# The beginning of a hybrid DeltaNet and attention layer: another order for scaled tiles, low parts, modulation rows and their weights

## The chip, the cores and the metric

The kernel runs on one core of one Trainium2 chip. The metric is the device time of one execution in microseconds (us). A median of three executions is given, and the profile of one execution. The engines are TensorE (PE, matrix products; PEld is its loading of the stationary operand), VectorE (DVE), ScalarE (ACT), GpSimd (POOL) and SyncE (SP, which issues most of the DMAs).

## The reference

One layer of a diffusion backbone over 1024 latent tokens and 256 context tokens, 1024 features wide. The part that the change touches is the start of it:

```
mod_x = silu(c) @ w_ada + b_ada          # shift, scale, gate, twice, for latent tokens
mod_c = silu(c_ctx) @ w_ada + b_ada      # the same for context tokens
px = modulate(rms_norm(x,   norm1_w), sh1,  sc1)  @ w_in
pc = modulate(rms_norm(ctx, norm1_w), csh1, csc1) @ w_in
# modulate(h, shift, scale) = h * (1 + scale) + shift
```

The columns of the projection feed a gated DeltaNet (convolution over the sequence, two scans) and a neighbourhood attention. Then come the output projection, a gated residual, a second modulated norm, and a SwiGLU network with its residual. All in float32.

## The kernel before, in words

The 1280 tokens (256 of context first) lie along the free dimension; the 1024 features are eight tiles `k` of 128 partitions. Float32 products are made from a high part (`hh` of the activations, `whi` of the weights, in the fast fp32r type) and a low part (`hl`, `wlo`, what the high part leaves), as three products: `hh` with `whi`, `hl` with `whi`, `hh` with `wlo`.

The beginning runs in these steps:

- SP loads the eight tiles `xt` (L680), the two raw weight blocks `fraw` for the first two projection blocks (L684), then the modulation weights `wada`, 1 MB for each tile (L676), and constants between them.
- The sums of squares go over ScalarE and VectorE to TensorE (L737 to L742), and `rs`, the inverse root, is made on ScalarE (L744, L745).
- `first[0].prefetch` casts and splits the first raw block on VectorE; `first[1].prefetch` the second on GpSimd (L201 the cast to `whi`, L204 the subtraction that gives `wlo`).
- `ada(j)` makes the modulation row of tile `j` on TensorE (L706: 16 instructions, four abreast) and copies it from PSUM to `arow` (L708). `column(j)` turns the row into columns by small products with `sel` (L714), adds the bias and makes the scale `w1s` on VectorE (L716, L719).
- `normed_tile(k)` scales the tile in place on VectorE (L726), makes `hh` on ScalarE, which adds the shift (L727), then `hl` on VectorE (L729). It does so in pieces: 256, 512 and 512 tokens for tile 0, 256 and 1024 for the others.
- The first two projection blocks (`first`, the DeltaNet's first two heads of k) are accumulated together, tile after tile (L757 for tile 0, L413 for the others), each over three PSUM banks. `AHEAD` says after which block of which tile a further row or column is made.

PE, DVE and ACT run this part in the order in which it is written (`tc.manual_schedule`); SP and POOL are in queues of their own. After tile 7 the third block begins outside that part, where the compiler's scheduler orders the engines: `first[0].evac()` copies the first block's three banks on ScalarE with a scale (L446) and VectorE adds the convolution's other taps straight from PSUM (L455); `jobs[2].prefetch()` casts the third block's weights on ScalarE (L203) and splits them on GpSimd (L204). The pool of `whi` and `wlo` has two buffers each, so the third block's take those of the first. Beside the later blocks VectorE accumulates another part of the modulation (L236, L238).

Of the kernel before, what the change touches and what calls it, by code (L numbers as in the profile page):

```python
# [9 lines left out]
F32 = mybir.dt.float32  # L10
# [3 lines left out]
AF = mybir.ActivationFunctionType  # L14
# [5 lines left out]
D, L, CT, T = 1024, 1024, 256, 1280  # L20
KT = 8
# [12 lines left out]
C_ID, C_LE, C_GE, C_BD2, C_ONE = range(5)  # L34
# [18 lines left out]
WIN = (256, 0)  # L53
CTX = {256: slice(0, 256), 0: slice(384, 640)}
PACE = 0.66
AHEAD = {(1, 0): (3,), (1, 1): (3, 4), (2, 0): (4, 5), (2, 1): (5, 6, 7), (3, 0): (6, 7)}
ORDER = [list(range(NCH)), [1, 0] + list(range(9, 1, -1))]


# [29 lines left out]
def hybrid(ctx, tc, a, dbg):  # L89
    nc = tc.nc  # L90
    pe, act, dve, pool, sp = nc.tensor, nc.scalar, nc.vector, nc.gpsimd, nc.sync
# [18 lines left out]
    bias = lasting("bias", [128, 8])  # L110
# [14 lines left out]
    M = [cst[:, i * 128:(i + 1) * 128] for i in range(4)] + [ones]  # L125
# [32 lines left out]
    mod1 = const("mod1", [128, 16, 2])  # L158
# [224 lines left out]
    with ExitStack() as bs:  # L383
# [7 lines left out]
        def bank(name="m"):  # L391

            if len(psum) == 1:
                return psum[0].tile([128, 512], F32, name=name, tag="ps")
            if len(psum) == 2:
                return psum[1].tile([128, 512], F32, name=name, tag=name, bufs=4 if name == "blk" else 2)
            return psum[2].tile([128, 512], F32, name=name, tag="ps", bufs=2)

        hh, hl = [], []
# [265 lines left out]
        first = [Block("k", 0), Block("k", 1)]  # L665
        with ExitStack() as xs:
            xp = pools(xs, "xp", "left")
            xt = []
            masks = xp.tile([128, 4, 128], F32, name="masks", tag="masks")
            ascope = ExitStack()  # L670
            wap = pools(ascope, "wap", "right", 7)
            aw = {}

            def load_ada(j):
                aw[j] = w = wap.tile([128, KT, 256], F32, name="wada", tag="wada")
                sp.dma_start(w, a["wa1"][j])  # L676

            for k in range(KT):
                x = xp.tile([128, T], F32, name=f"xt{k}", tag=f"xt{k}")
                sp.dma_start(x, a["xcT"][k])  # L680
                xt.append(x)
            raws = [xp.tile([128, KT, 128], F32, name=f"fraw{i}", tag=f"fraw{i}") for i in range(2)]
            for i in range(2):
                sp.dma_start(raws[i], a["w_conv"][4 + i])  # L684
            for j in range(3):
                load_ada(j)
            sp.dma_start(cst, a["cst"])
            sp.dma_start(masks, a["masks"])
            for j in range(3, KT):
                load_ada(j)  # L690
            sp.dma_start(cw, a["cw"])
            sp.dma_start(qkw, a["qkw"])
            sp.dma_start(onw, a["onw"])
            sp.dma_start(adt, a["adt"].rearrange("o d -> (o d)").partition_broadcast(128))
            wide = xp.tile([128, KT, 32], F32, name="wide", tag="wide")
            pool.memset(wide, 0.0)
            pool.tensor_copy(wide[:, :, 0:2], sc2)
            rs = xp.tile([128, T], F32, name="rs", tag="rs")
            rows = {}

            def ada(j, copy):

                p, w = bank("pm"), aw.pop(j)
                for k in range(KT):
                    s = slice(32 * (k % 4), 32 * (k % 4) + 32)
                    pe.matmul(p[s, :256], wide[:, k], w[:, k], start=k < 4, stop=k >= 4)  # L706
                rows[j] = xp.tile([128, 256], F32, name="arow", tag="arow", bufs=2)
                copy(rows[j], p[:, :256])  # L708

            def column(j):  # L710

                p, row = bank("pm"), rows.pop(j)
                for b in range(2):
                    pe.matmul(p[:, 2 * b:2 * b + 2], row[:, b * 128:(b + 1) * 128], sel, start=True, stop=True)  # L714
                m = mod1.rearrange("p (s b) c -> p s b c", s=2)[:, :, j]
                dve.tensor_tensor(m, p[:, 0:4].rearrange("p (s c) -> p s c", s=2),  # L716
                                  bada[:, 0:16].rearrange("p (s b) -> p s b", s=2)[:, :, j:j + 1].to_broadcast(
                                      [128, 2, 2]), OP.add)
                dve.tensor_scalar(w1s[:, j], m[:, 1], 1.0, n1w[:, j:j + 1], op0=OP.add, op1=OP.mult)  # L719

            def normed_tile(k, cuts=(slice(0, CT), slice(CT, T))):
                t = xt[k]
                parts = [(x, mod1[:, k, int(x.start < CT):int(x.start < CT) + 1]) for x in cuts]
                for x, sh in parts:
                    j = int(x.start < CT)
                    dve.scalar_tensor_tensor(t[:, x], t[:, x], w1s[:, k, j:j + 1], rs[:, x], op0=OP.mult, op1=OP.mult)  # L726
                    act.activation(hh[k][:, x], t[:, x], AF.Identity, bias=sh)  # L727
                for x, sh in parts:
                    dve.scalar_tensor_tensor(hl[k][:, x], t[:, x], sh, hh[k][:, x].bitcast(F32),  # L729
                                             op0=OP.add, op1=OP.subtract)  # L730

            with tc.manual_schedule(engines={mybir.EngineType.PE, mybir.EngineType.DVE, mybir.EngineType.Activation}):
                sums = [bank() for _ in SEGS]
                segs = [slice(s0, s0 + n) for s0, n in SEGS]
                for k in range(0, KT, 2):
                    sq = [xp.tile([128, T], F32, name="sq%d" % i, tag="sq%d" % i, bufs=2 + i) for i in range(2)]
                    act.activation(sq[0], xt[k], AF.Square)  # L737
                    for s in segs if k == KT - 2 else [slice(0, T)]:
                        act.activation(sq[1][:, s], xt[k + 1][:, s], AF.Square)
                        dve.tensor_tensor(sq[1][:, s], sq[0][:, s], sq[1][:, s], OP.add)  # L740
                    for p, s in zip(sums, segs):
                        pe.matmul(p[:, :s.stop - s.start], M[C_ONE], sq[1][:, s], start=k == 0, stop=k == KT - 2)  # L742
                for p, s in zip(sums, segs):
                    act.activation(rs[:, s], p[:, :s.stop - s.start], AF.Ln, bias=b_eps, scale=1.0 / D)  # L744
                act.activation(rs, rs, AF.Exp, scale=-0.5)  # L745
                first[0].prefetch(raws[0], dve, dve)
                first[1].prefetch(raws[1], pool, pool)
                ada(0, dve.tensor_copy)
                column(0)
                normed_tile(0, segs)  # L750
                ada(1, act.copy)
                for b in first:
                    b.banks()
                for j, (w, x) in enumerate(((0, hh), (1, hh), (0, hl))):
                    for b in first:
                        for o, s in b.outs:
                            pe.matmul(o, b.w[w][:, 0], x[0][:, s], start=j == 0, stop=False)  # L757
                        if j == 0 and b is first[1]:
                            column(1)
                            normed_tile(1)  # L760
                ada(2, act.copy)
                column(2)
                for k in range(1, KT):
                    if k == 3:
                        ascope.close()
                        h_tiles(pools(bs, "hp2", "right"), 4)
                    if k + 1 < KT:
                        normed_tile(k + 1)
                    for j, b in enumerate(first):
                        b.mm([k])  # L770
                        for q in AHEAD.get((k, j), ()):
                            if q in rows:
                                column(q)
                            else:
                                ada(q, act.copy)
                    if k == 5:
                        act.copy(mr[:, 4], ident)
                        act.copy(mr[:, 0:4], masks)
# [310 lines left out]
        for n in range(2, len(jobs) + 2):  # L1089
            j = jobs[n] if n < len(jobs) else None  # L1090
# [276 lines left out]
    parts = [[x[:, k] for k in range(4)] + [n[:, i] for n in na] for i, x in enumerate(ga)]  # L1367
# [130 lines left out]
    with ExitStack() as os_:  # L1498
# [21 lines left out]
        for b in range(2, KT - 2):  # L1520
            w, nxt = nxt, load_w(a["w_out"][b + 1], lo_engine=dve)
            sp.dma_start(x2[:, b], a["xcT"][b, :, CT:])
            outs = [bank(), bank()]
            for k in range(KT):
                for j, (wi, xi) in enumerate(((0, 0), (0, 1), (1, 0))):
                    for o, s in zip(outs, HV):
                        pe.matmul(o, w[wi][:, k], parts[xi][k][:, s], start=k == 0 and j == 0,  # L1527
                                  stop=k == KT - 1 and j == 2)
# [14 lines left out]
        for t, s in enumerate(HV):  # L1543
            outs = [bank(), bank()]
            last.append(outs)
            for k in range(KT):
                for j, (wi, xi) in enumerate(((0, 0), (0, 1), (1, 0))):
                    for o, w in zip(outs, ws):
                        pe.matmul(o, w[wi][:, k], parts[xi][k][:, s], start=k == 0 and j == 0,  # L1549
                                  stop=k == KT - 1 and j == 2)  # L1550
# [9 lines left out]
    with ExitStack() as us:  # L1560
# [66 lines left out]
        w = {}  # L1627
# [104 lines left out]
    for n, (wn, xn) in enumerate(zip(Stream.DOWN, FACTORS)):  # L1732
        o = chains[n in (1, 3, 5)]
# [90 lines left out]
```

## Time and profile before

| | us |
|---|---|
| median of 3 executions | 1516.04 |
| lowest, highest | 1512.98, 1517.41 |
| span of the profiled execution, first to last instruction | 1510.6 |
| own time of the profiled execution | not listed apart; its span stands for it |
| TensorE busy in it | 1462.2 |
| VectorE, ScalarE, GpSimd busy in it | 996.8, 703.5, 236.7 |

A row of the timeline gives the start in us from the first instruction, the duration, the engine, the line, the operation, the tiles written and read, the shape of the first one and the count of instructions merged into the row; in brackets the engine's idle time before it and what ended that. A row by stretches gives its length, the busy time of PE, PEld, DVE, ACT and POOL with counts of instructions, the granted share of TensorE's clock, the mean busy share of the DMA engines, and GB/s. A row of a group of instructions gives busy time, mean duration in ns, and idle time before with what ended it.

### The profile page before, as it was taken

What the parts mean: (1) busy time and instruction counts of PE and PEld (TensorE: products, weight loads), DVE (VectorE), ACT (ScalarE), POOL (GpSimd) and SP (SyncE); (2) the same over time, 40 slices, a digit from 0 to 9 for tenths busy, and PEclk for the clock granted to TensorE, in tenths of its full rate; (3) what the DMA queues carried; (4) which work ended last, traced back from release to release, by engine and by line L of the source; (5) the groups of instructions that cost most, each with busy time, mean ns of one, the idle gap of its engine ahead of it and who ended that gap; (6) DMA issues with size and microseconds to landing.
All of it is one profiled execution on the core that took longest, in us unless ns stands there. A gap on an engine that the chain in (4) does not pass through costs nothing.

```text
span 1510.6 us, 23890 instructions
## 1 busy us (share of the span) xinstructions
PE 1462.2 (97%) x8702; PEld 1223.5 (81%) x8702; DVE 996.8 (66%) x1716; ACT 703.5 (47%) x1389; POOL 236.7 (16%) x286
## 2 busy tenths in 40 slices
PE   6999999999999998999999999999999999999998
PEld 3788797877788877887878888888888888888887
DVE  5773589875463745778867389766665567598652
ACT  5453442456663246656853284333333334354440
POOL 1054601456652201111210000000000000000000
PEclk9999999999999999999999999999999999999999
DMA  9274122778665569998539205433333335798742
GB/s 389 75 215 143 54 78 72 244 222 248 195 191 174 157 187 291 290 263 279 163 112 343 79 28 166 141 105 105 105 105 105 105 105 174 260 360 279 251 140 84
DMA packets 205398, 267.36 MB, mean 177 GB/s; under 512 B 15968, under 2 KB 113760, under 8 KB 204256
## 3 DMA queue, kind: packets, MB, share of 16 engines
q1 hardware_dynamic: 197680, 260.01, 53.2%
q10 hardware_dynamic: 7600, 5.81, 1.2%
q8 instruction: 69, 1.13, 0.3%
q14 instruction: 49, 0.40, 0.1%
HBM read 201.02 MB, written 68.94 MB: 179 GB/s over the span
## 4 chain that ended last, share of the span: by engine, by line
PE 51%; ACT 1%; DVE 1%; issue 0%; DMA 0%; POOL 0%; DVEq 0%; POOLq 0%; ACTq 0%
PE ps L1398 28%; PE ps L1741 14%; PE ps L1527 3%; PE ps L1375 1%; PE ps L1549 1%; PE sc L332 1%; PE sc L322 1%; PE sc L309 1%; PE ps L1252 0%; PE ps L1261 0%; DMA z<-z_d 0%; ACT sq L1302 0%; ACT bt L315 0%; DVE bt L313 0%; PE ps L223 0%
## 5 line engine op out<-in xcount | busy, mean ns | idle before, releaser
L1459 ACT CAST uhi<-wq 128x512 fp32r<-128x512 f32 x101 | 61.3, 622 | 135.9 <-issue 84.6
L413 PE MATMUL blk<-hh,whi 128*128 128x512 f32 (+1 forms) x410 | 121.0, 389 | 1.6 <-ACT kk L562 1.4
L1459 ACT CAST uhi<-ws 128x512 fp32r<-128x512 f32 x91 | 54.0, 621 | 146.3 <-PE ps L1398 91.4
L413 PE MATMUL blk<-hl,whi 128*128 128x512 f32 (+1 forms) x410 | 113.4, 370 | 0.3 <-DVE hl L729 0.3
L609 PE MATMUL blk<-zw,hh 128*128 128x256 f32 (+1 forms) x576 | 112.3, 289 | 1.0 <-ACT cr L461 1.0
L413 PE MATMUL blk<-hh,wlo 128*128 128x512 f32 (+1 forms) x410 | 112.0, 370 | 0.6 <-POOL wlo L204 0.6
L1460 DVE TENSOR_TENSOR ulo<-wq,uhi 128x512 fp32r<-128x512 f32 x101 | 67.6, 688 | 59.1 <-ACT uhi L1459 32.7
L1398 PE MATMUL ps<-hT,uhi 128*128 128x512 f32 x336 | 103.7, 390 | 0.0
L1398 PE MATMUL ps<-lT,uhi 128*128 128x512 f32 x336 | 103.4, 389 | 0.0
L1398 PE MATMUL ps<-hT,ulo 128*128 128x512 f32 x336 | 103.4, 389 | 0.0
L609 PEld LDWEIGHTS blk<-zw,hh 128*128 128x128 f32 x576 | 90.7, 189 | 4.1 <-ACT cr L461 1.4
L1398 PE MATMUL ps<-hB,uhi 128*128 128x512 f32 x288 | 89.1, 390 | 0.0
L1398 PE MATMUL ps<-lB,uhi 128*128 128x512 f32 x288 | 88.7, 389 | 0.0
L1398 PE MATMUL ps<-hB,ulo 128*128 128x512 f32 x288 | 88.7, 389 | 0.0
L413 PEld LDWEIGHTS blk<-hh,wlo 128*128 128x128 f32 x410 | 71.0, 188 | 14.8 <-POOL wlo L204 0.9
L413 PEld LDWEIGHTS blk<-hl,whi 128*128 128x128 f32 x410 | 71.2, 188 | 14.4 <-DVE hl L729 0.8
L609 PE MATMUL blk<-zw,hl 128*128 128x256 f32 (+1 forms) x288 | 81.9, 284 | 0.0
L413 PEld LDWEIGHTS blk<-hh,whi 128*128 128x128 f32 x410 | 67.6, 190 | 16.8 <-issue 3.8
L204 POOL TENSOR_TENSOR wlo<-wraw,whi 128x1024 fp32r<-128x1024 f32 x18 | 44.8, 2488 | 186.8 <-ACT whi L203 186.5
L1398 PEld LDWEIGHTS ps<-lT,uhi 128*128 128x128 f32 x336 | 63.1, 188 | 13.1
L1398 PEld LDWEIGHTS ps<-hT,ulo 128*128 128x128 f32 x336 | 63.1, 188 | 13.1
L1398 PEld LDWEIGHTS ps<-hT,uhi 128*128 128x128 f32 x336 | 62.9, 188 | 13.0
(361 smaller groups left out, 3500.7 us busy)
## 6 DMA issues: line engine op xcount, KB each, us to landing
wq<-w_fo SPq DMA_DIRECT2D x99, 256.0 KB, 4.2
wq<-w_gu SPq DMA_DIRECT2D x88, 256.0 KB, 2.9
wad<-wa SPq DMA_DIRECT2D x64, 256.0 KB, 4.3
bt<-rpb SPq DMA_DIRECT2D x64, 192.0 KB, 3.9
t_d<-g SPq DMA_DIRECT2D x22, 512.0 KB, 3.5
fr<-t_d SPq DMA_DIRECT2D x44, 256.0 KB, 4.9
f_d<-g SPq DMA_DIRECT2D x33, 256.0 KB, 2.1
fr<-f_d SPq DMA_DIRECT2D x33, 256.0 KB, 4.2
```

The lines of the kernel that those rows point to most:

```text
L204: lo_engine.tensor_tensor(o, r, h.bitcast(F32), OP.subtract)
L309: s = pe.matmul(sc[:, u * 640 + n0:u * 640 + n1], q, ks[i], start=i == 0, stop=i == 1)
L322: pe.transpose(sc[:, u * 640 + j * 128:u * 640 + (j + 1) * 128], bt[:, j * 128:(j + 1) * 128], ident)
L332: pe.matmul(sc[u * ND:u * ND + ND, 1280:1408], vv, pt[:, j * 128:(j + 1) * 128], start=j == 0, stop=j == 4)
L413: pe.matmul(o, ww[:, k], xx[k][:, s], start=k == 0 and j == 0, stop=k == KT - 1 and j == 2)
L609: pe.matmul(p[:, :c1 - c0], x[k][:, s], ww[:, k, c0:c1], start=k == 0 and j == 0, stop=k == KT - 1 and j == 2)
L1375: pe.matmul(o, w[wi][:, k], parts[xi][k][:, s], start=k == 4 and j == 0, stop=k == 3 and j == 2)
L1398: pe.matmul(o, w[wi][:, k], x[xi][:, k], start=first and k == 0 and j == 0, stop=k == n - 1 and j == 2, skip_group_check=True)
L1459: act.copy(hi, self.raw[key])
L1460: dve.tensor_tensor(lo, self.raw[key], hi.bitcast(F32), OP.subtract)
L1527: pe.matmul(o, w[wi][:, k], parts[xi][k][:, s], start=k == 0 and j == 0, stop=k == KT - 1 and j == 2)
L1741: pe.matmul(o[b], w[wi][:, b], F[xn, p][xi], start=n in (0, 1, 5) and p == 0 and j == 0, stop=p == NFB // 2 - 1 and j == 2, skip_group_che ...
```

## The change

In SP's queue the first modulation weights are loaded ahead of the two raw weight blocks. `ada` takes a tuple of tiles and writes up to two rows into one PSUM bank, with one copy; tiles 4 and 5, and 6 and 7, are done by twos. `normed_tile` is split into `high` (scaling and `hh`) and `low` (`hl`); from tile 2 on, the next tile's `high` stands ahead of the present tile's `low`. The six groups of three products of a tile are in a new order: all four that need `hh` first, the two that need `hl` last. `busy(n)` issues n products of `ones` with a tile of squares into a bank that nobody reads, three between row 0 and column 0, two after column 0. The table `AHEAD` gives way to `behind`, which names a group instead of a block.

```diff
             raws = [xp.tile([128, KT, 128], F32, name=f"fraw{i}", tag=f"fraw{i}") for i in range(2)]
+            load_ada(0)
             for i in range(2):
                 sp.dma_start(raws[i], a["w_conv"][4 + i])
-            for j in range(3):
+            for j in (1, 2):
                 load_ada(j)
...
+            def ada(js, copy):
+
+                p = bank("pm")
+                for n, j in enumerate(js):
+                    w = aw.pop(j)
+                    for k in range(KT):
+                        s = slice(32 * (k % 4), 32 * (k % 4) + 32)
+                        pe.matmul(p[s, n * 256:n * 256 + 256], wide[:, k], w[:, k], start=k < 4, stop=k >= 4)
+                row = xp.tile([128, 512], F32, name="arow", tag="arow", bufs=2)
+                copy(row[:, :len(js) * 256], p[:, :len(js) * 256])
...
+            def high(k, cuts=whole):
                 t = xt[k]
+                for x in cuts:
                     j = int(x.start < CT)
                     dve.scalar_tensor_tensor(t[:, x], t[:, x], w1s[:, k, j:j + 1], rs[:, x], op0=OP.mult, op1=OP.mult)
+                    act.activation(hh[k][:, x], t[:, x], AF.Identity, bias=shifted(k, x))
+
+            def low(k, cuts=whole):
+                for x in cuts:
+                    dve.scalar_tensor_tensor(hl[k][:, x], xt[k][:, x], shifted(k, x), hh[k][:, x].bitcast(F32),
                                              op0=OP.add, op1=OP.subtract)
+
+            def part(b, k, w, x):
+                for o, s in b.outs:
+                    pe.matmul(o, b.w[w][:, k], x[k][:, s], start=k == 0 and w == 0 and x is hh,
+                              stop=k == KT - 1 and x is hl)
+
+            def busy(n):
+
+                for _ in range(n):
+                    pe.matmul(idle[:, :256], M[C_ONE], sq[0][:, :256], start=True, stop=True)
...
                 first[0].prefetch(raws[0], dve, dve)
                 first[1].prefetch(raws[1], pool, pool)
-                ada(0, dve.tensor_copy)
+                ada((0,), dve.tensor_copy)
+                busy(3)
                 column(0)
-                normed_tile(0, segs)
-                ada(1, act.copy)
+                busy(2)
+                high(0, segs)
+                low(0, segs)
+                ada((1,), act.copy)
                 for b in first:
                     b.banks()
...
+                one, two = first
+                part(one, 0, 0, hh)
+                column(1)
+                high(1)
+                part(one, 0, 1, hh)
+                part(two, 0, 0, hh)
+                part(two, 0, 1, hh)
+                ada((2,), act.copy)
+                part(one, 0, 0, hl)
                 column(2)
+                part(two, 0, 0, hl)
+                low(1)
+                high(2)
+                behind = {(1, 0): lambda: ada((3,), act.copy), (1, 2): lambda: column(3),
+                          (2, 2): lambda: ada((4, 5), act.copy), (2, 4): lambda: (column(4), column(5)),
+                          (2, 5): lambda: ada((6, 7), act.copy), (3, 3): lambda: (column(6), column(7))}
                 for k in range(1, KT):
...
-                    if k + 1 < KT:
-                        normed_tile(k + 1)
-                    for j, b in enumerate(first):
-                        b.mm([k])
-                        for q in AHEAD.get((k, j), ()):
...
+                    if k >= 2 and k + 1 < KT:
+                        high(k + 1)
+                    if k >= 2:
+                        low(k)
+                    for n, (b, w, x) in enumerate(((one, 0, hh), (one, 1, hh), (two, 0, hh), (two, 1, hh),
+                                                   (one, 0, hl), (two, 0, hl))):
+                        part(b, k, w, x)
+                        if (k, n) in behind:
+                            behind[k, n]()
```

More of the change, by code (lines that the diff above doesn't have):

```diff
@@ L699, in hybrid @@
             rows = {}
[L701 to L708, printed above, removed]
+            def ada(js, copy):
[7 more added lines that the diff above has]
+                copy(row[:, :len(js) * 256], p[:, :len(js) * 256])
+                for n, j in enumerate(js):
+                    rows[j] = row[:, n * 256:n * 256 + 256]
             def column(j):
@@ L719, in column, with shifted @@
                 dve.tensor_scalar(w1s[:, j], m[:, 1], 1.0, n1w[:, j:j + 1], op0=OP.add, op1=OP.mult)
-            def normed_tile(k, cuts=(slice(0, CT), slice(CT, T))):
+            whole = (slice(0, CT), slice(CT, T))
+            def shifted(k, x):
+                return mod1[:, k, int(x.start < CT):int(x.start < CT) + 1]
+            def high(k, cuts=whole):
                 t = xt[k]
-                parts = [(x, mod1[:, k, int(x.start < CT):int(x.start < CT) + 1]) for x in cuts]
-                for x, sh in parts:
+                for x in cuts:
                     j = int(x.start < CT)
                     dve.scalar_tensor_tensor(t[:, x], t[:, x], w1s[:, k, j:j + 1], rs[:, x], op0=OP.mult, op1=OP.mult)
-                    act.activation(hh[k][:, x], t[:, x], AF.Identity, bias=sh)
-                for x, sh in parts:
-                    dve.scalar_tensor_tensor(hl[k][:, x], t[:, x], sh, hh[k][:, x].bitcast(F32),
+                    act.activation(hh[k][:, x], t[:, x], AF.Identity, bias=shifted(k, x))
+            def low(k, cuts=whole):
+                for x in cuts:
+                    dve.scalar_tensor_tensor(hl[k][:, x], xt[k][:, x], shifted(k, x), hh[k][:, x].bitcast(F32),
                                              op0=OP.add, op1=OP.subtract)
+            def part(b, k, w, x):
[5 more added lines that the diff above has]
+                    pe.matmul(idle[:, :256], M[C_ONE], sq[0][:, :256], start=True, stop=True)
             with tc.manual_schedule(engines={mybir.EngineType.PE, mybir.EngineType.DVE, mybir.EngineType.Activation}):
@@ L745, in hybrid @@
                 act.activation(rs, rs, AF.Exp, scale=-0.5)
+                idle = bank()
                 first[0].prefetch(raws[0], dve, dve)
                 first[1].prefetch(raws[1], pool, pool)
-                ada(0, dve.tensor_copy)
+                ada((0,), dve.tensor_copy)
+                busy(3)
                 column(0)
-                normed_tile(0, segs)
-                ada(1, act.copy)
+                busy(2)
+                high(0, segs)
+                low(0, segs)
+                ada((1,), act.copy)
                 for b in first:
                     b.banks()
[L754 to L761, printed above, removed]
-                column(2)
+                one, two = first
[7 more added lines that the diff above has]
+                part(one, 0, 0, hl)
+                column(2)
+                part(two, 0, 0, hl)
[4 more added lines that the diff above has]
+                          (2, 5): lambda: ada((6, 7), act.copy), (3, 3): lambda: (column(6), column(7))}
                 for k in range(1, KT):
@@ L766, in hybrid @@
                         h_tiles(pools(bs, "hp2", "right"), 4)
-                    if k + 1 < KT:
-                        normed_tile(k + 1)
-                    for j, b in enumerate(first):
-                        b.mm([k])
-                        for q in AHEAD.get((k, j), ()):
[L772 to L775, printed above, removed]
+                    if k >= 2 and k + 1 < KT:
[7 more added lines that the diff above has]
+                            behind[k, n]()
                     if k == 5:
```

1 line of the change is left out of this document (removed).

## The prediction

> **What bounds the kernel now.** I read the page first, then the busy time by stretches of 10 and of 1 us over the beginning, then the timeline of the first 100 us. The page's head and its table of engines say that TensorE (PE) sets the pace:
>
> ```profile
> span 1510.6 us, 23890 instructions
> PE 1462.2 (97%) x8702; PEld 1223.5 (81%) x8702; DVE 996.8 (66%) x1716; ACT 703.5 (47%) x1389; POOL 236.7 (16%) x286
> ```
>
> TensorE sits idle for 48 us of the whole span, so what the change can win lies where TensorE waits or runs slowly in the edited stretch, from the first modulation row (21.8 us) to the first product of the third block (67.6 us). In the stretches of 1 us below, the number before the last two is the granted clock.
>
> ```profile
> 21.00:22.00 1.00, 0.24 (x5) 0.19 (x8) 0.58 (x1) 0.88 (x2) 1.00 (x1) 1.00 1.02 426
> 23.00:24.00 1.00, 0.58 (x4) 0.52 (x4) 0.37 (x1) 0.08 (x1) 0.80 (x1) 1.00 1.04 434
> 24.00:25.00 1.00, 0.81 (x9) 0.40 (x12) 0.80 (x4) 0.00 (x0) 0.00 (x0) 0.55 0.95 393
> 30.00:31.00 1.00, 1.00 (x5) 0.81 (x5) 0.96 (x3) 0.27 (x1) 0.00 (x0) 0.54 1.00 418
> ```
>
> TensorE is 0.24 and 0.58 busy, then the clock is halved just after 24.0 and comes back just before 31. The first products of the two blocks, from 26.1 on, run at half speed: 4.9 us that would take 2.4. That is the most the filler sums can win. The DMA engines are full (share about 1.0), at some 420 GB/s.
>
> **The change part by part.** The rows of the start, from the timeline (start, duration, engine, line; in brackets the idle time before and what ended it):
>
> ```profile
> 18.92 0.69 DVE L201 CAST whi<-fraw 128x1024 fp32r<-128x1024 f32 x1
> 19.24 1.26 POOL L201 CAST whi<-fraw 128x1024 fp32r<-128x1024 f32 x1 [13.63 <-DMA fraw<-w_conv]
> 19.64 1.94 DVE L204 TENSOR_TENSOR wlo<-fraw,whi 128x1024 fp32r<-128x1024 f32 x1
> 21.81 1.07 PE L706 MATMUL pm<-wada,wide 128*32 128x256 f32 x16 [0.76 <-DMA wada<-wa]
> 22.94 0.42 DVE L708 COPY arow<-pm 128x256 f32<-128x256 f32 x1 [1.36 <-PE pm L706]
> 23.42 0.61 PE L714 MATMUL pm<-bias,arow 128*128 128x2 f32 x4 [0.54 <-DVE arow L708]
> 24.22 1.94 PE L706 MATMUL pm<-wada,wide 128*32 128x256 f32 x16 [0.19 <-DMA wada<-wa]
> 24.59 1.81 DVE L726 SCALAR_TENSOR_TENSOR xt<-xt,w1s,rs 128x256 f32<-128x256 f32 x3
> 25.77 1.38 ACT L727 ACTIVATE hh<-xt,mod 128x512 fp32r<-128x512 f32 x2 [0.15 <-DVE xt L726]
> ```
>
> *First modulation weights sooner.* No transfer is added; the first `wada` (1 MB) passes the two `fraw` (0.5 MB each) on SP's queue, and later ones keep their places. `wada` 0 and 1 land 2.4 us apart (21.81, 24.22), so 1 MB costs 2.4 us: `wada` 0 lands near 19.3 instead of 21.8, both `fraw` 2.4 us later, the second near 21.65, the first half of that earlier, near 20.45. The row product can now start when the sums of squares leave TensorE, near 21.0, 0.8 us sooner. But VectorE does `whi` and `wlo` of the first block ahead of the row's copy: 0.69 from 20.45, then `wlo` for 1.1 to 1.9, to 22.3–23.1, and the copy 0.42. TensorE puts three filler sums between row and column; the row product's 16 instructions run four abreast in about a microsecond (rows below), some 0.22 for a pass of 256 columns, two passes to an f32 sum, so 1.3 for three. The column starts near 23.3, 0.1 sooner than now: the gain is nothing. What is late next is the second block's weights on GpSimd (POOL). Its cast goes from about 21.7 to 23.1, and `wlo` follows. Whether that matters is read from later rows of the same engines:
>
> ```profile
> 66.63 2.39 POOL L204 TENSOR_TENSOR wlo<-wraw,whi 128x1024 fp32r<-128x1024 f32 x1 [42.83 <-ACT whi L203]
> 81.02 2.88 POOL L602 TENSOR_TENSOR zw<-wraw,zw 128x1088 fp32r<-128x1088 f32 x1 [4.47 <-ACT zw L601]
> 81.43 0.75 DVE L455 SCALAR_TENSOR_TENSOR cacc<-blk,cw,cacc 128x512 f32<-128x512 f32 x1
> 82.09 2.36 DVE L238 SCALAR_TENSOR_TENSOR acc<-wad,sc,acc 128x512 f32<-128x512 f32 x1
> 85.03 0.73 DVE L238 SCALAR_TENSOR_TENSOR acc<-wad,sc,acc 128x512 f32<-128x512 f32 x1
> 92.99 3.52 DVE L238 SCALAR_TENSOR_TENSOR acc<-wad,sc,acc 128x512 f32<-128x512 f32 x1
> 93.02 2.96 POOL L566 TENSOR_TENSOR kd<-kk,cst 128x1280 f32<-128x1280 f32 x1 [0.88 <-ACT kk L562]
> ```
>
> The accumulation at L238 reads two SBUF tensors. Alone it takes 0.73; beside a GpSimd product it ends 0.5 us after that product does (82.09+2.36 against 81.02+2.88; 92.99+3.52 against 93.02+2.96). The form that reads PSUM (81.43) isn't held. So GpSimd's `wlo`, 23.2 to 25.6 after the change, holds VectorE's first scaling of tile 0, which reads `xt` and `rs` from SBUF: its first piece ends near 26.15 instead of 25.07, 1.1 us later. The other end is no hold, 0. I take 1.1; three rows stand nearest.
>
> [...]
>
> *Filler sums.* Five, 2.1 us on TensorE, in time when it waits for VectorE or ScalarE. They fill the idle stretches ahead of the drop, so I take the clock to stay up. The other end, that it falls all the same, is a rival.
>
> *Tiles scaled ahead of low parts, rows by twos.* This moves instructions in three hand-written queues, so the cost is where a queue stands. The durations, first from the groups of instructions of the first 70 us by shape (busy, mean ns, idle before), then from the timeline:
>
> ```profile
> L729 DVE SCALAR_TENSOR_TENSOR hl<-xt,mod,hh 128x1024 fp32r<-128x1024 f32 x7 | 9.0, 1285 | 5.5 <-ACT hh L727 5.5
> L727 ACT ACTIVATE hh<-xt,mod 128x1024 fp32r<-128x1024 f32 x7 | 8.0, 1150 | 3.7 <-DVE xt L726 3.7
> L708 ACT COPY arow<-pm 128x256 f32<-128x256 f32 x7 | 2.6, 367 | 7.9 <-PE pm L706 7.9
> 56.40 1.67 DVE L726 SCALAR_TENSOR_TENSOR xt<-xt,w1s,rs 128x256 f32<-128x256 f32 x2
> 58.17 0.75 PE L413 MATMUL blk<-hh,whi 128*128 128x256 f32 x3
> 58.76 0.75 PE L413 MATMUL blk<-hl,whi 128*128 128x256 f32 x3
> 39.53 0.50 PE L714 MATMUL pm<-bias,arow 128*128 128x2 f32 x4
> 39.96 1.07 PE L706 MATMUL pm<-wada,wide 128*32 128x256 f32 x16
> 40.96 0.85 PE L413 MATMUL blk<-hh,whi 128*128 128x256 f32 x3
> 46.55 1.93 PE L706 MATMUL pm<-wada,wide 128*32 128x256 f32 x32
> ```
>
> From start to start: a group of three products 0.585 (58.17 to 58.76), six groups to a tile, 3.5; a column 0.43; a row product 1.0, two 1.9. VectorE now waits 5.5 us for `hh` ahead of the low parts; with the next tile's scaling in between that goes, and its 3.3 us a tile (scaling 1.67, low part as much) hide under 3.5 of TensorE. But ScalarE copies a row only after the `hh` halves queued before it, and the columns wait for the rows. The chain, on the new order: `hh` of tile 0 ends at 27.15+1.1 = 28.25; copy of row 1, 0.37; from a column's start to the scaling 1.17 (23.42 to 24.59); scaling of tile 1, 1.67; its `hh` 1.15; copy of row 2, 0.37; column 2 to VectorE's next piece 1.17; low part of tile 1 and scaling of tile 2, 3.3; `hh` 1.15; copy of row 3, 0.37. Column 3 starts near 39.0. TensorE, from column 2 at 33.0 on, has 0.43, four groups and a row product ahead of it, is there by 36.8 and waits some 2.1 us, with the rest of tile 1 queued behind. Now there is no such wait: row 3's copy has only tile 2's first half ahead of it that is late, and column 3 runs at 39.53 without idling.
>
> From column 3: 0.43, three groups 1.75, tile 2 with four rows by twos and two columns 3.5+3.8+0.9, tile 3 with two columns 4.4, tiles 4 to 7 14.0 and some 0.3 for a low part just late. The third block's turn comes at 68.1, against 67.64: +0.5. Without GpSimd's hold, −0.6; without the wait for column 3 too, −2.7.
>
> *Hand-over to the third block.* The rows:
>
> ```profile
> 64.73 0.74 PE L413 MATMUL blk<-hl,whi 128*128 128x512 f32 x2 [0.34 <-DVE hl L729]
> 65.51 1.05 ACT L203 CAST whi<-wraw 128x1024 fp32r<-128x1024 f32 x1 [1.75 <-PE blk L413]
> 66.46 3.14 ACT L446 ACTIVATE cacc<-blk,cw 128x256 f32<-128x256 f32 x6
> 67.64 0.51 PE L413 MATMUL blk<-hh,whi 128*128 128x256 f32 x2
> 69.07 0.62 PE L413 MATMUL blk<-hh,wlo 128*128 128x256 f32 x2 [0.57 <-POOL wlo L204]
> ```
>
> The third block's `whi` needs the first block's buffer. Its last reader, the low part's product, ends at 65.47, 2.2 ahead of the turn; then come the cast 1.05, GpSimd's `wlo` 2.39, and TensorE still waits 0.57. After the change that reader is the last group but one, ending 0.4 ahead of the turn: everything is 1.75 later. The cast is done 0.7 after the turn, a bare loss, unless something hides it; `wlo` is late by up to 1.75, less if products that need `whi` alone fill in. So 0.7 to 1.75 with the cast first. But the first block's three evacuations come free at the same moment as the buffer: ahead of the cast, they add half of 3.14, up to 3.3. I take 1.8.
>
> Sum: +0.5 +1.8 = +2.3 us, on a span of 1510.6. The median run, 1516.04, lies 5.4 above that span (other executions, and what lies around the span), so **1518.3**, 0.15% slower: no change that can be told, the bound for that being 0.3%, 4.5 us. A shift reaches the end: TensorE is 97% busy.
>
> **The rivals.** *Slower:* all six evacuations go ahead of the third block's cast on ScalarE. That adds 3.14 to 1.75, 4.9 at the hand-over, 1521.4 with the 0.5; it decides from a hand-over loss of 4.0 on. For it: both blocks now end within 0.6 us. Against: the cast stands between them in program order.
>
> *Clock falls all the same:* tile 0's products wait till 26.7 with only fillers and one row product before. Up to 2.4 us more, less what the chain over ScalarE and VectorE hides: 1518–1520.7.
>
> [...]
>
> *Faster:* no hold, no wait for column 3 (−2.7), a hand-over at its lowest (+0.7), and a later wait gone with it, from the list of waits (total, times, longest in us):
>
> ```profile
> PE m L537 <- DVE cacc L455: 1.7, 1, 1.7
> ```
>
> That makes −3.7, 1512.3; past 0.3% (below 1511.5) only if the hand-over costs nothing as well. Against it: ScalarE's queue is strictly the written one.
>
> **How the numbers follow.** The forecast 0.47, with its own range 1515.5–1520; no hold 0.12; clock falls 0.10; six evacuations 0.16; the faster case 0.15. Slower by over 0.3% (above 1520.6): the six evacuations and a part of the clock case, 0.20. Faster (below 1511.5): 0.12. Within: 0.68. The range leaves out about 0.1 each side: 1512 to 1522.
>
> **What would show it.** Right: granted clock 1.00 from 20 to 32; GpSimd's `wlo` from `fraw` ending near 25.6, the scaling of tile 0 beside it over 1 us long; TensorE idle about 2 us ahead of column 3, ended by `arow`; the third block's cast after 67 and TensorE idle 2 to 4 us there; VectorE's 5.5 us of waits for `hh` gone. Wrong: `wlo` done before the scaling, column 3 without a wait, or a cast that starts before the second block is nearly done.

## The result and the profile after

The changed kernel takes 1518.03 us (median of 17 runs, 1516.18 to 1523.18), the kernel before 1514.08 beside it on the same chip (17 runs, 1510.88 to 1517.41). The ratio is 1.0024, its 95% interval 1.0014 to 1.0034: 0.24% slower, below the 0.3% that the prediction set as its bound, but the interval excludes equality. The profiled execution took 1516.18, with a span of 1514.3 against 1510.6: 3.7 us, where 2.3 were forecast. Three executions, one of run 6 and two of run 7, took 2076 to 8263 us and are left out of the medians below.

The head of the page and its table of engines, after:

```profile
span 1514.3 us, 23899 instructions
PE 1465.3 (97%) x8712; PEld 1225.3 (81%) x8712; DVE 994.4 (66%) x1716; ACT 703.1 (46%) x1387; POOL 235.8 (16%) x286
```

TensorE is busy for 3.1 us more, 2.7 of them in ten more products: the five filler sums, 1.56 and 1.11 us in the timeline below. Up to TensorE's last product the time at half clock is the same in sum, 10.2 us (before: 24.10 to 30.93 and 293.75 to 297.17; after: 72.76 to 76.17, 263.90 to 267.32 and 298.04 to 301.45), but it has moved. The stretches of 10 us show that the clock now stays up at the start (the number before the last two; before, it was halved from 24.1 to 30.9):

```profile
20.00:30.00 10.00, 8.97 (x63) 5.49 (x62) 7.83 (x15) 5.04 (x8) 3.91 (x2) 1.00 1.02 421
30.00:40.00 10.00, 8.49 (x66) 5.35 (x65) 5.61 (x12) 3.83 (x6) 0.00 (x0) 1.00 1.02 402
70.00:80.00 10.00, 8.52 (x36) 6.84 (x35) 10.00 (x19) 4.78 (x6) 4.50 (x2) 0.83 0.24 76
```

The third row shows the price: now the clock falls at the hand-over to the third block. The timeline of the start, after (first row product, three filler sums, GpSimd's `wlo`, column 0, two filler sums, the scale, the first scaling, column 3):

```profile
21.37 1.07 PE L708 MATMUL pm<-wada,wide 128*32 128x256 f32 x16
22.37 1.56 PE L750 MATMUL m<-sq,ones 128*128 128x256 f32 x6
23.07 2.35 POOL L203 TENSOR_TENSOR wlo<-fraw,whi 128x1024 fp32r<-128x1024 f32 x1
23.77 0.50 PE L718 MATMUL pm<-bias,arow 128*128 128x2 f32 x4
24.14 1.11 PE L750 MATMUL m<-sq,ones 128*128 128x256 f32 x4
24.51 0.93 DVE L723 TENSOR_SCALAR w1s<-mod,prm 128x2 f32<-128x2 f32 x1
25.54 1.81 DVE L734 SCALAR_TENSOR_TENSOR xt<-xt,w1s,rs 128x256 f32<-128x256 f32 x3
38.44 0.61 PE L718 MATMUL pm<-bias,arow 128*128 128x2 f32 x4 [1.48 <-ACT arow L710]
```

The scaling of tile 0 starts at 25.54 instead of 24.59, and TensorE stands for 1.48 us ahead of column 3. Then the hand-over, from the last group of tile 7 on:

```profile
66.75 1.34 PE L744 MATMUL blk<-hl,whi 128*128 128x256 f32 x6
67.08 1.63 ACT L445 ACTIVATE cacc<-blk,cw 128x256 f32<-128x256 f32 x3 [4.54 <-PE blk L744]
68.59 1.05 ACT L202 CAST whi<-wraw 128x1024 fp32r<-128x1024 f32 x1
69.69 0.61 PE L412 MATMUL blk<-hh,whi 128*128 128x256 f32 x2 [1.60 <-ACT whi L202]
69.72 2.37 POOL L203 TENSOR_TENSOR wlo<-wraw,whi 128x1024 fp32r<-128x1024 f32 x1 [44.30 <-ACT whi L202]
72.14 0.62 PE L412 MATMUL blk<-hh,wlo 128*128 128x256 f32 x2 [1.48 <-POOL wlo L203]
```

ScalarE does three evacuations, then the cast; TensorE waits 1.60 for it, does the four products that need `whi` alone, and waits 1.48 for GpSimd. Before, the same place cost 0.57. By stretches cut at the waits and at the drop (length, then TensorE's busy time; the clock is the number after the counts):

```profile
69.30:72.70 3.40, 1.53 (x7) 1.11 (x8) 3.40 (x7) 1.87 (x4) 2.37 (x1) 1.00 0.27 82
72.76:76.17 3.41, 3.41 (x12) 2.73 (x11) 3.41 (x7) 0.00 (x0) 0.00 (x0) 0.50 0.51 154
```

TensorE is busy for 1.53 us in 3.40, and the next 3.41 us run at half clock: up to 1.7 us more that the waits cost. The clock falls there in all five traces with both long waits (after and runs 2 to 5) and in none of the five with a wait of 0.57.

How the loss travels is seen by products that both kernels have. First the timeline of before, then that of after:

```profile
140.60 0.85 PE L413 MATMUL blk<-hh,whi 128*128 128x256 f32 x3 [1.39 <-ACT kk L562]
259.89 0.42 PE L922 MATMUL m<-cst,N 80*128 80x80 f32 x2 [1.29 <-DVE N L915]
261.35 0.70 PE L413 MATMUL blk<-hh,whi 128*128 128x512 f32 x2
```

```profile
143.36 0.85 PE L412 MATMUL blk<-hh,whi 128*128 128x256 f32 x3 [1.39 <-ACT kk L561]
262.81 0.42 PE L953 MATMUL m<-cst,N 80*128 80x80 f32 x2 [1.30 <-DVE N L946]
264.33 1.20 PE L412 MATMUL blk<-hh,whi 128*128 128x512 f32 x2
```

The shift is 2.05 us at the third block's first product (69.69 against 67.64), 3.07 at its first `wlo` product (72.14 against 69.07), then up to 1.7 more by the clock; the wait of 1.7 us for `cacc` that before has at 99 us is gone, and what is left at 141 us is 2.76, at 260 us 2.92. The last rows show the rest: two products take 1.20 us that took 0.70 in before. The clock is halved there from 263.90 to 267.32, in this execution and not in that of before, which brings the account up to about the 3.7 of the span. That drop comes and goes between executions: run 6, which is before with three filler sums, has it at 260.16, and run 4 lacks it.

### The profile page after: what moved, and what is told of

Same layout as the page of the kernel before. It is cut to its first block, busy times and chain, and to the rows that moved or that the text cites. A ratio compares the mean times of both kernels' runs of the same rounds, so it can differ in the third digit from the quotient of the medians.

```text
span 1514.3 us, 23899 instructions
## 1 busy us (share of the span) xinstructions
PE 1465.3 (97%) x8712; PEld 1225.3 (81%) x8712; DVE 994.4 (66%) x1716; ACT 703.1 (46%) x1387; POOL 235.8 (16%) x286
## 4 chain that ended last, share of the span: by engine, by line
PE 51%; ACT 1%; DVE 1%; DMA 0%; issue 0%; POOL 0%; DVEq 0%; POOLq 0%; ACTq 0%
PE ps L1429 28%; PE ps L1772 14%; PE ps L1558 3%; PE ps L1406 1%; PE ps L1580 1%; PE sc L331 1%; PE sc L321 1%; PE sc L308 1%; DMA z<-z_d 0%; PE ps L1283 0%; PE ps L1292 0%; ACT sq L1333 0%; ACT bt L314 0%; DVE bt L312 0%; PE ps L222 0%
## 5 line engine op out<-in xcount | busy, mean ns | idle before, releaser
L412 PE MATMUL blk<-hh,whi 128*128 128x512 f32 (+1 forms) x368 | 111.0, 394 | 3.1 <-ACT whi L202 1.6
L412 PE MATMUL blk<-hl,whi 128*128 128x512 f32 (+1 forms) x368 | 104.0, 375 | 0.0
L412 PE MATMUL blk<-hh,wlo 128*128 128x512 f32 (+1 forms) x368 | 102.4, 374 | 1.5 <-POOL wlo L203 1.5
L412 PEld LDWEIGHTS blk<-hh,wlo 128*128 128x128 f32 x368 | 64.7, 191 | 14.7 <-POOL wlo L203 1.8
L412 PEld LDWEIGHTS blk<-hl,whi 128*128 128x128 f32 x368 | 65.2, 191 | 12.7
L412 PEld LDWEIGHTS blk<-hh,whi 128*128 128x128 f32 x368 | 61.3, 191 | 16.2 <-issue 2.2
```

The source lines that it names most:

```text
L412: pe.matmul(o, ww[:, k], xx[k][:, s], start=k == 0 and j == 0, stop=k == KT - 1 and j == 2)
```

## The experiments

All were timed beside the kernel before. The table stands here to be looked up; "turn" is TensorE's time from the first scaling of tile 0 to the point where it is ready for the third block (start of the block's first product less its wait), which leaves out that executions begin some tenths apart. It also leaves out what delays that first scaling, so the early weights and GpSimd's hold don't show in it. The turn of run 2 has a stretch at half clock in it, 29.45 to 32.86, that after doesn't have.

| kernel | ratio to before (interval) | turn, us | hand-over waits, us |
|---|---|---|---|
| before | 1 | 43.05 | 0.57 |
| after | 1.0024 (1.0014 to 1.0034) | 42.55 | 1.60 + 1.48 |
| 1 old order in the last tile | 0.9996 (0.9985 to 1.0006) | 42.39 | 0.57 |
| 2 cast written first | 1.0032 (1.0018 to 1.0046) | 43.73 | 1.02 + 1.98 |
| 3 raw blocks first | 1.0022 (1.0010 to 1.0033) | 42.57 | 1.60 + 1.48 |
| 4 rows 2 and 3 together | 1.0024 (1.0012 to 1.0037) | 40.71 | 1.60 + 1.48 |
| 5 no filler sums | 1.0039 (1.0025 to 1.0054) | 43.96 | 1.60 + 1.48 |
| 6 before with filler sums | 0.9986 (0.9975 to 0.9996) | 41.36 | 0.57 |
| 7 all mended | 0.9972 (0.9956 to 0.9988) | 40.54 | 0.57 |
| 8 order and rows mended | 0.9983 (0.9970 to 0.9996) | 40.54 | 0.57 |

**1. The old order of groups in the last tile alone.** The theory is that the hand-over is the whole loss; the rival, that the loss lies in the start or the clock elsewhere.

```diff
+                    groups = ((one, 0, hh), (one, 1, hh), (two, 0, hh), (two, 1, hh), (one, 0, hl), (two, 0, hl))
+                    if k == KT - 1:
+                        groups = ((one, 0, hh), (one, 0, hl), (one, 1, hh), (two, 0, hh), (two, 0, hl), (two, 1, hh))
-                              stop=k == KT - 1 and x is hl)
+                              stop=k == KT - 1 and w == 1)
```

> The changed kernel with tile 7's six groups in the old order (a block's high, low and wlo groups together), all else as changed. Theory (the loss lies at the hand-over, because the first block's whi buffer and its banks come free together, one group before the end): the third block's cast starts about 2 us ahead of the turn again, TensorE's waits there fall from 1.60 + 1.48 us to under 1, the clock is not halved at 73 us, the turn itself stays near 67.9, and the whole gains 3 to 4 us over the changed kernel, so at most 0.05% above the kernel before. Rival (the loss comes from the order inside the beginning, the wait for column 3 and GpSimd's hold, and the hand-over is paid back by the wait at 99 us that is gone): under 1 us gained, still 0.2% above before.

Measured: 1512.51 (11 runs, 1511.14 to 1517.91), ratio 0.9996. The timeline of this kernel:

```profile
66.54 1.05 ACT L202 CAST whi<-wraw 128x1024 fp32r<-128x1024 f32 x1 [3.25 <-PE blk L744]
67.49 3.15 ACT L445 ACTIVATE cacc<-blk,cw 128x256 f32<-128x256 f32 x6
68.69 0.51 PE L412 MATMUL blk<-hh,whi 128*128 128x256 f32 x2
70.11 0.61 PE L412 MATMUL blk<-hh,wlo 128*128 128x256 f32 x2 [0.57 <-POOL wlo L203]
```

The cast is 2.15 us ahead of the turn, the evacuations go behind it, the wait is 0.57 as before, and the clock stays up. All else of the change is still there, and the loss is gone: with the change's order in the last tile the ratio is 1.0024, without it 0.9996, and the intervals don't meet. The hand-over is the cause. The run moves two things there at once, the release of the buffer and the cast's place ahead of the evacuations.

**2. The cast written ahead of the evacuations.** It asks whether the evacuations, or the late release of the buffer, make the two waits.

```diff
-        first[0].evac()
         jobs[2].prefetch()
+        first[0].evac()
```

> The changed kernel with the third block's prefetch written ahead of the first block's evacuation, so that the scheduler puts the cast ahead of the third evacuating copy (it was behind all three). Theory: the cast starts some 0.5 us sooner (one 512-wide copy less ahead), TensorE's first wait at the hand-over falls from 1.60 to about 1.1 and the second stays near 1.5; less than 1 us gained in all, which shows that the buffer's late release, not the copies, is the larger part. Rival (the copies are the cause): the wait nearly goes and 2 us or more are gained.

Measured: 1519.02 (8 runs), ratio 1.0032. The timeline of this kernel:

```profile
68.64 1.05 ACT L445 ACTIVATE cacc<-blk,cw 128x256 f32<-128x256 f32 x2 [4.53 <-PE blk L744]
69.58 1.04 ACT L202 CAST whi<-wraw 128x1024 fp32r<-128x1024 f32 x1
70.67 0.62 PE L412 MATMUL blk<-hh,whi 128*128 128x256 f32 x2 [1.02 <-ACT whi L202]
70.70 2.86 POOL L203 TENSOR_TENSOR wlo<-wraw,whi 128x1024 fp32r<-128x1024 f32 x1 [44.90 <-DVE cacc L454]
73.62 0.85 PE L412 MATMUL blk<-hh,wlo 128*128 128x256 f32 x2 [1.98 <-POOL wlo L203]
```

The scheduler still lets two of three evacuations pass first. The first wait falls by the one evacuation, 0.6, and the second rises by 0.5, since GpSimd's subtraction takes 2.86 instead of 2.37 (why was not tested). The two waits are 3.0 in sum either way, so taking one copy out of the cast's way gained nothing. It doesn't separate the copies' share from that of the late release, since two copies still stand ahead of the cast: in after the three held it from 67.08 to 68.59, 1.51 us, here the two held it from 68.64 to 69.58.

**3. The raw weight blocks ahead of the first modulation weights again.** It asks what the earlier weights brought, and what GpSimd's lateness cost.

```diff
-            load_ada(0)
             for i in range(2):
                 sp.dma_start(raws[i], a["w_conv"][4 + i])
-            for j in (1, 2):
+            for j in range(3):
```

> The changed kernel with the two raw weight blocks loaded ahead of the first modulation weights again. Theory (GpSimd's product holds VectorE): GpSimd's wlo of the second block ends before 24, w1s takes 0.23 instead of 0.93 us, the first scaling of tile 0 starts near 24.9 instead of 25.54 although the weights come 2.5 us later, and the turn to the third block comes 0.6 us sooner; with the hand-over unchanged the whole gains about 0.6. Rival (the early weights do help): the scaling starts later than 25.54 and the whole loses 0.5 to 1 us.

Measured: 1517.32 (12 runs), ratio 1.0022. The timeline of this kernel:

```profile
21.01 3.22 POOL L203 TENSOR_TENSOR wlo<-fraw,whi 128x1024 fp32r<-128x1024 f32 x1
22.26 1.07 PE L707 MATMUL pm<-wada,wide 128*32 128x256 f32 x16 [0.71 <-DMA wada<-wa]
23.26 1.56 PE L749 MATMUL m<-sq,ones 128*128 128x256 f32 x6
24.66 0.50 PE L717 MATMUL pm<-bias,arow 128*128 128x2 f32 x4
25.39 0.23 DVE L722 TENSOR_SCALAR w1s<-mod,prm 128x2 f32<-128x2 f32 x1
25.72 1.81 DVE L733 SCALAR_TENSOR_TENSOR xt<-xt,w1s,rs 128x256 f32<-128x256 f32 x3
```

GpSimd is done at 24.23, and the scale `w1s` takes 0.23 instead of 0.93: the hold is gone. But the first scaling starts at 25.72, not sooner: the row product waits for its weights, 22.26 instead of 21.37, and the column follows as much later, 24.66 instead of 23.77. The expected gain is a miss: what the hold cost in after, the late weights cost instead, and the turn and the time are those of after. In other executions the hold is longer or shorter (below), so this balance is that of these two traces. The rows also show the filler sums in the way: they end the column's wait, not the row's copy. The copy, at 23.38 for 0.42, is done 0.86 us ahead of the column; in before (22.94 and 0.42, column at 23.42) it was 0.06.

**4. Rows 2 and 3 as one pair.** It takes away the copy of row 3 that stands behind tile 2's `hh` on ScalarE.

```diff
-                ada((2,), act.copy)
+                ada((2, 3), act.copy)
                 part(one, 0, 0, hl)
...
-                behind = {(1, 0): lambda: ada((3,), act.copy), (1, 2): lambda: column(3),
+                behind = {(1, 2): lambda: column(3),
```

> The changed kernel with rows 2 and 3 made together and copied once, instead of row 3 in a copy behind tile 2's hh. Theory (column 3 waits for the copy that stands behind tile 2's hh on ScalarE): the wait of 1.48 us ahead of column 3 goes, column 2 comes up to 1 us later because the pair takes longer on TensorE, and the turn to the third block comes 1 to 2 us sooner, near 66.5; the whole gains about that. Rival (VectorE and ScalarE set the pace of tiles 1 and 2 anyway): the wait turns up ahead of tile 2's or 3's products and the turn stays within 0.5 us of 67.9.

Measured: 1518.84 (12 runs, 1513.07 to 1520.47), ratio 1.0024. The timeline of this kernel:

```profile
36.18 0.50 PE L718 MATMUL pm<-bias,arow 128*128 128x2 f32 x4
67.70 0.62 PE L412 MATMUL blk<-hh,whi 128*128 128x256 f32 x2 [1.60 <-ACT whi L202]
70.14 1.01 PE L412 MATMUL blk<-hh,wlo 128*128 128x256 f32 x2 [1.48 <-POOL wlo L203]
```

Column 3 starts without a wait, and the third block's first product comes 2.0 us sooner than in after. The trace shows the gain, the timed median doesn't; the lowest run, 1513.07, is 3 us below the lowest of after. Taken by itself this run leaves the worth in time open; run 8 bears on it.

**5. No filler sums.**

```diff
                 ada((0,), dve.tensor_copy)
-                busy(3)
                 column(0)
-                busy(2)
```

> The changed kernel without the five filler sums (the output is the same). Theory (the fillers keep the clock up, but the chain over ScalarE and VectorE hides most of what that is worth here): the clock falls to 0.5 near 24 to 27 us and comes back 3.4 or 6.8 us later, the turn to the third block, from the first scaling of tile 0, is 1.0 to 1.5 us later, and the whole loses about 1 us against the changed kernel. Rival (full worth): the turn is 2.4 us later or more.

Measured: 1520.29 (9 runs), ratio 1.0039; the interval overlaps that of after. First two stretches of 5 us of this kernel, then two rows of its timeline:

```profile
25.00:30.00 5.00, 3.07 (x22) 1.78 (x15) 4.73 (x7) 2.15 (x4) 1.18 (x1) 0.59 1.01 412
30.00:35.00 5.00, 5.00 (x32) 3.52 (x32) 2.07 (x4) 2.04 (x3) 0.00 (x0) 0.73 1.01 421
```

```profile
23.83 2.35 POOL L203 TENSOR_TENSOR wlo<-fraw,whi 128x1024 fp32r<-128x1024 f32 x1
24.27 1.93 DVE L723 TENSOR_SCALAR w1s<-mod,prm 128x2 f32<-128x2 f32 x1
```

The clock falls as in before, and the turn is 1.4 us later than in after. So here the filler sums do hold the clock, and that is worth 1.4 at the turn, not the 2.4 that half speed takes from the products; that the chain over VectorE and ScalarE hides the rest is argued, not shown. They don't hold it in every execution: run 2 has all five, and its clock fell at 29.45. The two rows belong to the hold, below.

**6. The kernel before with three filler sums, and nothing else of the change.**

```diff
                 ada(0, dve.tensor_copy)
+                busy(1)
                 column(0)
+                busy(2)
```

> The kernel before with three filler sums added, one between row 0 and column 0 and two behind column 0, nothing else changed. Theory: the clock stays at 1.00 from 20 to 32 us, the turn to the third block comes 1.5 to 2 us sooner than 67.64 and the hand-over stays as it is, so the whole is 1.5 to 2 us (0.1%) faster than before: the fillers were the part of the change that pays. Rival (what is won at the clock is lost again at a later wait on VectorE): the turn comes sooner but the whole stays within 0.5 us.

Measured: ratio 0.9986, interval 0.9975 to 0.9996 (the median of eleven runs is 1512.57). A stretch, and then a row of the timeline of this kernel:

```profile
25.00:30.00 5.00, 4.60 (x35) 2.93 (x34) 4.28 (x10) 2.15 (x4) 0.00 (x0) 1.00 1.01 412
```

```profile
68.03 0.61 PE L413 MATMUL blk<-hh,wlo 128*128 128x256 f32 x2 [0.57 <-POOL wlo L204]
```

The clock stays up, and the first `wlo` product of the third block starts 1.0 us sooner than in before, 1.7 counted from the first scaling. One filler sum ahead of the column and two behind it were enough in this execution.

**7 and 8. What the runs point to.** Run 7 has the edits of 1, 3 and 4, with one filler sum ahead of the column and four behind it. Run 8 has the edits of 1 and 4 only, so that it keeps the early weights and the fillers as they were.

```diff
-                busy(3)
+                busy(1)
                 column(0)
-                busy(2)
+                busy(4)
```

> The changed kernel with its three costs taken out together: tile 7's groups in the old order, the raw weight blocks ahead of the first modulation weights, rows 2 and 3 in one copy; one filler ahead of column 0 and four behind it. Theory: no halved clock before 200 us, no wait ahead of column 3, TensorE's wait at the hand-over 0.57; the turn comes 3 us sooner than the changed kernel's, and the whole is 2 to 4 us (0.2%) faster than before. Rival: VectorE or ScalarE sets the pace of the later tiles, the turn comes less than 1.5 us sooner, and the whole is level with before.

> As the run with three costs taken out, but with the first modulation weights still ahead of the raw blocks and the fillers as in the change: tile 7's groups in the old order, and rows 2 and 3 in one copy. Theory (GpSimd's hold costs 0.6 to 1 us): the whole is that much slower than that run, about 1.5 to 2.5 us faster than before. Rival (the early weights cost nothing): level with that run.

Measured: run 7 has ratio 0.9972 (median of ten runs 1510.95, lowest 1507.55), run 8 0.9983 (12 runs, median 1512.14, lowest 1508.62). Both are faster than either kernel. TensorE's waits from 15 to 110 us, in full (total, times, longest), first of run 7, then of run 8:

```profile
PE blk L412 <- POOL wlo L203: 0.6, 1, 0.6
PE pm L707 <- DMA wada<-wa: 0.3, 1, 0.3
```

```profile
PE blk L744 <- ACT hh L735: 1.9, 3, 1.2
PE blk L412 <- POOL wlo L203: 0.6, 1, 0.6
```

The waits for column 3 and for the cast are gone in both. By the table the turn comes 2.0 us sooner than in after, where 3 were expected of run 7. Run 8 still waits for tile 0's `hh`, behind the hold by GpSimd; run 7 doesn't. The two runs differ in the place of the filler sums as well as in the early weights, by 0.1% in the ratio, and their intervals overlap: what the early weights cost, if anything, is open. Run 8 against run 1 differs by the pair of rows 2 and 3: 0.9983 against 0.9996, 2 us, as run 4's trace had it; these intervals overlap too.

## Why the prediction was right

*The forecast* was 1518.3, 0.15% slower and not to be told from no change; it is 1518.03, 0.24% slower. That the two times lie 0.3 us apart is luck: the forecast started from the 1516.04 of three runs, 2.0 above the 1514.08 measured beside the changed kernel, and its loss of 2.3 us was 1.4 to 1.7 too small (3.7 by the spans, 3.95 by the medians). By step:

*First modulation weights, forecast to gain nothing: right.* The row product started at 21.37 (21.0 forecast), the column at 23.77 (23.3; the three filler sums took 1.56 on TensorE, not 1.3, and the column waited for them).

*GpSimd's hold, forecast 1.1 by the L238 rows: right in kind, wrong in its victim, and its size is no fixed one.* The first scaling came 0.95 later. But what was held was the instruction ahead of it, the scale `w1s` of two elements: it ends at 25.44 (24.51 and 0.93), GpSimd's `wlo` at 25.42 (23.07 and 2.35). In run 5, without fillers, it took 1.93 and ended at 26.20, `wlo` at 26.18; in run 3, with `wlo` done sooner, 0.23. So the hold was 0.70 in after, and the rest of the 0.95 came with the later column. In the other runs with early weights `w1s` took 0.54 to 1.80, each time to 0.02 after the end of `wlo`: how long the hold is depends on when `wlo` ends beside column 0, and that differs between executions. Like the scaling, it reads two tensors in SBUF. The Trainium skill, "SBUF — State Buffer", section "SBUF: two separate sides", says that a Vector instruction with two SBUF inputs shares an exclusive lock with a GpSimd instruction that reads SBUF, and that the later one is blocked whole: the rows agree, to 0.02 us. The case without a hold falls.

*Filler sums, forecast to keep the clock up: right in this execution* (1.00 from 20 to 40). The clock fell early in both traces without them (before and run 5) and stayed up in seven of the eight with them; in run 2 it fell at 29.45.

*Column 3, forecast start 39.0 and wait 2.1: right in kind*, 38.44 and 1.48; run 4 removes it. VectorE's 5.5 us of waits for `hh` ahead of the low parts are gone, as forecast. *The turn*, forecast 68.1: 68.09 (69.69 less its wait of 1.60). The match hides two misses of 0.6 that cancel: column 3 came that much sooner, and from its start to the turn TensorE took 29.65 us, where 29.1 were summed.

*Hand-over, 1.8 taken: this is the mis-sized term.* The mechanism, a buffer released at the turn, was right, and with the old order in the last tile (run 1) the loss is gone. But half of the evacuations went ahead of the cast, the case that the prediction priced at "up to 3.3" and kept for the range, and the products with `whi` alone didn't shorten the sum. The waits measured 3.08 against 0.57, 2.5 more. Not foreseen at all: the two waits also halved the clock for 3.41 us. That this didn't show as a total of over 4 is due to the wait at 99 us, 1.7 in before, which the prediction gave to the faster case alone as one that may go with it. It went here too, and it is gone in every trace with the changed order of tiles, run 1 included, while run 6 still has 1.4 of it; why was not tested.

*The rival with all six evacuations ahead* didn't occur: three are ahead in the timeline, three behind. *The faster rival* needed no hold and no wait for column 3: both were there.

## What to carry to other kernels

An order that puts the last reader of a weight buffer at the end of a tile showed no cost in the earlier tiles (turn 40.54 in run 8, 41.36 in run 6) and cost 0.28% in the last one (run 1 against after): there the release of the buffer starts the next block's cast and split, so end with groups that the next block doesn't wait for. When products are reordered, ask of each buffer which instruction is now its last reader, and what is queued on the engine that refills it. Filler work that keeps the clock up should not stand ahead of the chain that it covers: three sums ahead of the column made it start 0.86 us after its row's copy was done (run 3). One ahead and four behind went with the lowest ratio here, though not told apart from three and two.

## What the runs showed of the hardware

The clock fell after waits that were each short: 1.60 and 1.48 us at the hand-over, 0.76 and less at the start of before. It fell only at certain moments: within each of the ten traces the falls lie whole multiples of 3.413 us apart (in before 24.10 and 293.75, 79 steps; in after 72.76, 263.90 and 298.04, 56 and 10 steps). These moments lie elsewhere in each execution: 24.10 in before and 72.76 in after are 14.26 steps apart. One such step of before, one of run 1 and one of run 2, by stretches:

```profile
20.69:24.10 3.41, 2.04 (x21) 1.02 (x20) 1.35 (x3) 2.19 (x3) 3.11 (x1) 1.00 1.00 416
24.48:27.89 3.41, 2.04 (x21) 0.83 (x19) 3.31 (x4) 0.92 (x2) 1.69 (x1) 1.00 1.04 422
26.03:29.44 3.41, 2.55 (x24) 1.40 (x17) 3.41 (x6) 2.15 (x4) 0.00 (x0) 1.00 1.06 431
```

After the first and the third the clock fell; after the second it stayed, with TensorE as busy in it as in the first (2.04 us). So no long gap is needed, and TensorE's busy time in the step doesn't decide alone; what else does, the rows don't settle. The Trainium skill, "TensorE: Matmul & The Clock Gate", section "What's actually happening", gives a free-running window of 3413 ns; the steps agree, and so do the halved stretches, which measure 3.41 and 6.83 us, one and two of them. The advice of the Trainium skill, same page, section "Why this matters for your kernels", to avoid idle gaps of over about 3 us is too mild for this kernel: the drops at the hand-over and at the start came at gaps of about half that or less.

The spread between runs of one kernel goes with the mean granted clock of the run. Of the 17 runs of after, the four at 0.996 took 1516.2 to 1516.9, the four at 0.993 1520.1 to 1521.6, the one at 0.992 1523.2: about 1.3 us for each 0.001, by a line through all 17. Differences of 2 us between medians therefore depend on where in a long kernel the drops happen to fall. Run 4 is the case: its gain of 1.8 us at the turn doesn't show in its median, while its mean, 1517.7, lies 1.0 below the 1518.6 of after at the same mean clock, 0.995. Whether the gain is worth 1 or 2 us is not settled by it.
